# Two pairs of the first block taken plainly, weight buffers in another order, and four banks for the last pieces of a SwiGLU block

## The chip, the cores and the metric

The kernel runs on one core of one Trainium2 chip. The metric is the time of one execution on the device in microseconds (us); lower is better. All times of the trace are counted from the start of the profiled span.

## The reference

Two layers of a decoder trunk over 256 tokens of width 2048, in float32. Layer 0 mixes tokens with an mLSTM, layer 1 with a gated linear recurrence (RG-LRU); each layer then has a SwiGLU feed-forward block of width 5632.

```python
def swiglu(x, w_in, w_out):
    g, u = jnp.split(x @ w_in, 2, axis=-1)
    return (jax.nn.silu(g) * u) @ w_out

    h = x
    for layer in range(DEPTH):
        hn = rms_norm(h, norm_mix[layer])
        ...
        h = h + mix
        h = h + swiglu(rms_norm(h, norm_ffn[layer]), ffn_w_in[layer], ffn_w_out[layer])
    return rms_norm(h, norm_final)
```

## The kernel before, in words

**Products.** Every float32 operand is split into a high part and a rest, `hi` and `lo` (ACT casts `hi`, DVE subtracts to get `lo`: lines 229 and 230, or 208 and 209 in the mixers). One product is three matmuls, hi·hi, hi·lo and lo·hi (lines 725 to 727 in `ffn`, 281 to 283 in `linear_tok`).

**The feed-forward block.** `ffn` walks over 11 blocks `j` of 512 columns of the gate and of the up weights. Each block has 8 pairs `p` of k-tiles. Pairs 0, 1, 4 and 7 are plain: 8 products, so 24 matmuls of 128x512. Pairs 2, 3, 5 and 6 (`SEVENS`) use a scheme with seven products, 21 matmuls, for which DVE first makes sums of the weights (`sum`, lines 265 to 269) and two sets of operands are split (`whix`/`wlox` from the raw weights, `whit`/`wlot` from the sums). So a plain pair takes one buffer each of `whi` and `wlo`, a seven-product pair two of each. There are three buffers each of `raw`, `whi` and `wlo`, taken in turn by `four`, and one of `sum`. A cast into a buffer waits until the last matmul on what it held before is done.

**The output.** The result of block `j` is transposed (`tv`, line 780, split into `hh`), and multiplied with 512 rows of `ffn_w_out` in eight pieces (`outs`), 12 matmuls each, which are put between the matmuls of the following block from its pair 3 on. A piece uses one PSUM bank, `out`: ACT copies `h` into it (line 816), TensorE adds on top, ACT copies it back (line 823). In block 0 no pieces stand in between, since there is no block behind it.

**End of a layer.** Four pieces of block 9 are left over when block 10's products end. They run with the transposes of block 10 and the start of `project_out`, which multiplies block 10 with the last rows of `ffn_w_out` as a plain projection (`po0` to `po3`, lines 281 to 283), adds to `h` on DVE (line 458) and has ACT square the new columns (`junk`, line 334). Behind layer 0 the RG-LRU mixer follows: its first product `rec` (lines 298 to 300) needs its weights split by ACT (line 208) and DVE (line 209).

**What sets the order.** Within an engine the order is the program's, decided when the kernel is built by a scheduler that follows priorities (`tc.high_priority` draws work ahead) and the freeing of buffers. `PLACES` lists the buffers as memory pools in the order in which they are laid out; the pools of the next stage are laid over them from the front, and wait for whatever lies there.

## Time and profile before

| | |
|---|---|
| time, median of 3 runs | 2143.91 us (2141.2 to 2144.5) |
| profiled execution: its own time | 2139.45 us |
| profiled execution: span | 2137.6 us |
| TensorE (PE) busy | 2103.3 us, 98% of the span |
| VectorE (DVE) busy | 1595.6 us, 75% |
| ScalarE (ACT) busy | 1282.6 us, 60% |
| read from memory | 401.84 MB at 189 GB/s |

The profiled execution took 1.85 us more than its span, and 4.46 us less than the median of the runs. A row of a timeline gives the start in us, the duration, the engine, the line of the kernel, the operation and its operands, and in brackets how long the engine was idle before it and which instruction it then waited for. PE is TensorE's matmuls, PEld its weight loads, SPq the queue that issues transfers.

### The profile page before, as it was taken

To read this page: it belongs to the slowest core of one execution; us is meant where nothing else is said; L and a number is where in the kernel's file an instruction comes from. 1 tells how busy PE (TensorE), PEld (TensorE's weight loads), DVE (VectorE), ACT (ScalarE), POOL (GpSimd) and SP (SyncE) were. 2 spreads that over 40 slices of the span, in tenths; PEclk is the share of its full clock that TensorE was granted. 3 is DMA by queue.
4 is the path that set the end of the run, shared out by engine and by line. 5 is a ranking of instruction groups with operands and counts; after the bars stand their busy time and mean duration, and the time that the engine had idled before them with its cause. 6 is when DMAs were issued, how large, how long until landed. Compare 5 with 4: busy or idle time off the path is not lost.

```text
span 2137.6 us, 27324 instructions
## 1 busy us (share of the span) xinstructions
PE 2103.3 (98%) x10592; PEld 1774.7 (83%) x10592; DVE 1595.6 (75%) x1612; ACT 1282.6 (60%) x1458; POOL 43.0 (2%) x62
## 2 busy tenths in 40 slices
PE   9999999999999999999989999999999999999997
PEld 8988888777888888888879999777788888888886
DVE  6655556688788787878756786768877878887874
ACT  5344445556666656666654758655666666666664
POOL 0011110000000000000000000000000000000001
PEclk9999999999999999999999999999999999999999
DMA  6556656455665565665526665746566555566652
GB/s 212 168 160 183 179 179 223 160 197 197 204 215 193 187 206 179 213 219 195 181 97 195 191 189 186 228 156 203 192 210 221 191 184 196 194 206 211 207 181 105
DMA packets 211082, 405.73 MB, mean 190 GB/s; under 512 B 14520, under 2 KB 14728, under 8 KB 210824
## 3 DMA queue, kind: packets, MB, share of 16 engines
q1 hardware_dynamic: 210808, 402.94, 58.4%
q8 instruction: 83, 1.36, 0.3%
q10 hardware_dynamic: 144, 1.05, 0.1%
q14 instruction: 47, 0.39, 0.0%
HBM read 401.84 MB, written 2.10 MB: 189 GB/s over the span
## 4 chain that ended last, share of the span: by engine, by line
PE 91%; DVE 3%; ACT 3%; issue 1%; DMA 1%; SPq 0%; POOL 0%; ACTq 0%; POOLq 0%; DVEq 0%
PE P L725 7%; PE P L726 7%; PE P L727 7%; PE out L725 6%; PE out L727 6%; PE out L726 6%; PE Q L726 6%; PE Q L725 6%; PE Q L727 6%; PE po L282 3%; PE po L281 3%; PE po L283 3%; PE qk L298 1%; PE qk L299 1%; PE rec L300 1%; PE qk L300 1%
## 5 line engine op out<-in xcount | busy, mean ns | idle before, releaser
L209 DVE TENSOR_TENSOR wlo<-raw,whi 128x1024 fp32r<-128x1024 f32 (+1 forms) x225 | 273.0, 1218 | 183.8 <-ACT whi L208 182.8
L208 ACT CAST whi<-raw 128x1024 fp32r<-128x1024 f32 (+1 forms) x225 | 234.3, 1047 | 207.7 <-PE po L283 47.0
L230 DVE TENSOR_TENSOR wlot<-sum,whit 128x2048 fp32r<-128x2048 f32 x88 | 201.7, 2292 | 143.7 <-ACT whit L229 143.6
L725 PE MATMUL out<-whio,hh 128*128 128x512 f32 x640 | 249.9, 390 | 1.7 <-ACT out L816 1.7
L727 PE MATMUL out<-whio,hh 128*128 128x512 f32 x640 | 249.1, 389 | 0.0
L726 PE MATMUL out<-wloo,hh 128*128 128x512 f32 x640 | 249.1, 389 | 0.0
L823 ACT COPY h<-out 128x512 f32<-128x512 f32 x158 | 92.5, 586 | 259.0 <-PE out L727 258.8
L230 DVE TENSOR_TENSOR wlo<-raw,whi 128x2048 fp32r<-128x2048 f32 x96 | 220.2, 2296 | 32.1 <-ACT whi L229 31.2
L229 ACT CAST whio<-rawo 128x1024 fp32r<-128x1024 f32 x160 | 168.8, 1055 | 122.4 <-PE out L727 120.1
L229 ACT CAST whit<-sum 128x2048 fp32r<-128x2048 f32 x88 | 168.3, 1912 | 69.7 <-DVE sum L269 34.0
L229 ACT CAST whi<-raw 128x2048 fp32r<-128x2048 f32 x96 | 184.0, 1917 | 30.7 <-PE P L727 16.4
L230 DVE TENSOR_TENSOR wloo<-rawo,whio 128x1024 fp32r<-128x1024 f32 x160 | 193.3, 1221 | 8.8 <-ACT whio L229 8.3
L230 DVE TENSOR_TENSOR wlox<-raw,whix 128x1536 fp32r<-128x1536 f32 x88 | 154.5, 1756 | 50.3 <-ACT whix L229 49.9
L725 PEld LDWEIGHTS out<-whio,hh 128*128 128x128 f32 x640 | 120.1, 188 | 28.9 <-ACT out L816 4.0
L229 ACT CAST whix<-raw 128x1536 fp32r<-128x1536 f32 x88 | 130.4, 1482 | 20.5 <-PE Q L727 10.3
L727 PEld LDWEIGHTS out<-whio,hh 128*128 128x128 f32 x640 | 120.2, 188 | 25.2
L726 PEld LDWEIGHTS out<-wloo,hh 128*128 128x128 f32 x640 | 120.2, 188 | 24.9
L725 PE MATMUL Q<-whi,p_f 128*128 128x512 f32 x352 | 139.3, 396 | 0.9 <-DVE ds L764 0.9
L726 PE MATMUL Q<-wlo,p_f 128*128 128x512 f32 x352 | 137.5, 391 | 1.7 <-DVE wlo L230 1.7
L725 PE MATMUL P<-whi,p_f 128*128 128x512 f32 x352 | 137.8, 392 | 0.3 <-DVE ds L765 0.2
L727 PE MATMUL P<-whi,p_f 128*128 128x512 f32 x352 | 137.3, 390 | 0.0
L727 PE MATMUL Q<-whi,p_f 128*128 128x512 f32 x352 | 137.2, 390 | 0.0
(273 smaller groups left out, 4960.9 us busy)
## 6 DMA issues: line engine op xcount, KB each, us to landing
raw<-in_ffn_w_in_dram SPq DMA_DIRECT2D x352, 512.0 KB, 4.8
rawo<-in_ffn_w_out_dram SPq DMA_DIRECT2D x160, 512.0 KB, 4.2
raw<-in_m_w_in_dram SPq DMA_DIRECT2D x95, 512.0 KB, 3.8
raw<-in_r_w_in_dram SPq DMA_DIRECT2D x64, 512.0 KB, 4.1
raw<-in_m_w_out_dram SPq DMA_DIRECT2D x32, 512.0 KB, 3.8
raw<-in_r_w_out_dram SPq DMA_DIRECT2D x32, 512.0 KB, 4.3
raw<-in_ffn_w_out_dram SPq DMA_DIRECT2D x16, 512.0 KB, 6.3
gr<-in_r_gate_w_dram SPq DMA_DIRECT2D x8, 512.0 KB, 3.8
```

The costliest lines, as they stand in the source:

```text
L208: nc.scalar.copy(hi[:, i:i + step, 0:ncols], r)
L209: nc.vector.tensor_tensor(lo[:, i:i + step, 0:ncols], r, hi[:, i:i + step, 0:ncols].bitcast(F32), op=ALU.subtract)
L229: nc.scalar.copy(hi, src)
L230: nc.vector.tensor_tensor(lo, src, hi.bitcast(F32), op=ALU.subtract)
L281: nc.tensor.matmul(o, lhsT=ah[:, bs], rhs=hi, start=(k == 0), stop=False)
L282: nc.tensor.matmul(o, lhsT=ah[:, bs], rhs=lo, start=False, stop=False)
L283: nc.tensor.matmul(o, lhsT=al[:, bs], rhs=hi, start=False, stop=(k == nk - 1))
L300: nc.tensor.matmul(o, lhsT=lo, rhs=ah, start=False, stop=last, skip_group_check=True)
L725: nc.tensor.matmul(o, lhsT=a[0], rhs=b[0], start=start, stop=False, **kw)
L726: nc.tensor.matmul(o, lhsT=a[0], rhs=b[1], start=False, stop=False, **kw)
L727: nc.tensor.matmul(o, lhsT=a[1], rhs=b[0], start=False, stop=stop, **kw)
L823: nc.scalar.copy(hs, o)
```

## The change

Three edits. **(1)** In block 0 of each layer pairs 2 and 3 (`BOTH`) are taken plainly. The activations' three extra operands for each of the two (`more`, tags `m2` and `m3`) are made in `pair`, beside those of the seven products, during the projection ahead of the block. The pool of `h1` is opened only when `more` is closed, behind block 0; the early buffers change with it: pair 0 now takes `raw0`, `whi0` and `wlo0`, pair 1 takes memory of `h0` and `ds`. **(2)** `PLACES` is put in another order. **(3)** The pieces behind the first two left over, and all eight of block 10, are taken with `last=True`: weights come as one buffer of four k-tiles through `four` with two `raw` buffers in turn, the sum starts fresh in one of four banks (`acc`: Q5, P2, Q3, P4), and DVE adds it to `h`. This takes the place of `project_out`. The next norm is opened ahead of the pieces of block 10.

```diff
+BOTH = (2, 3)
...
     PLACES = (
-        "raw1", "raw2", "sum0", "whi1", "wlo1", "whi2", "rawo", "whio", "wloo", "wlo2", "raw0", "whi0", "wlo0",
+        "raw1", "raw2", "sum0", "rawo", "whio", "wloo", "wlo1", "whi1", "wlo2", "whi2", "raw0", "whi0", "wlo0",
     )
...
+    def is_plain(j, p):
+        return p not in SEVENS or j == 0 and p in BOTH
...
-            if p not in SEVENS:
+            if is_plain(j, p):
                 with tc.high_priority(offset=AHEAD):
                     both = halves(f"{j}_{p}", raw)
...
+            if p in BOTH:
+
+                nc.scalar.copy(c[:, 8, :], c[:, 0, :])
+                nc.vector.tensor_tensor(c[:, 9, :], c[:, 1, :], c[:, 2, :], op=ALU.subtract)
+                nc.vector.tensor_tensor(c[:, 10, :], c[:, 3, :], c[:, 0, :], op=ALU.subtract)
+                more = pool_of("more").tile([P, 2, 3, P], F32R, tag=f"m{p}", name=f"m{p}_{self.name}")
+                split(more[:, 0], more[:, 1], c[:, 8:11, :])
+                self.more[p] = more
...
-        early.update(raw="h0", whi="h1", wlo="ds")
+        early.update(raw=[None, "h0"], whi=[None, "ds"])
...
-            def load(q):
+            def load(q, last):
                 tiles.clear()
+                if last:
+                    raw = four("raw", f"o{j}{q}", F32, 2)
+                    for i in (0, 2):
+                        nc.sync.dma_start(raw[:, i:i + 2, :], wv[:, i:i + 2, q * NB:(q + 1) * NB])
+                    with tc.high_priority(offset=AHEAD):
+                        tiles.extend(halves(f"o{j}{q}", raw))
+                    return
...
-                o = pool_of("out").tile([P, NB], F32, tag="out", name=f"out{j}{q}{b}")
-
-
-                first = fresh.pop() if fresh else False
+                name = f"out{j}{q}{b}"
+                o = acc(name) if last else pool_of("out").tile([P, NB], F32, tag="out", name=name)
+
+
+                first = last or fresh.pop() if last or fresh else False
...
-        for left in range(len(work)):
-            work.pop(0)()
-            if left > 0 and turns:
+        turn["raw"] %= 2
+        for i, (piece, q, b) in enumerate(work):
+            piece(q, b, i >= 2)
+            if i >= len(work) - 2:
                 turns.pop(0)()
-        project_out(
-            ffn_w_out[layer][(NJ - 1) * NB:, :], 4, lambda k: (hi[:, k, :], lo[:, k, :]), nxt,
-        )
+        nxt.open()
+        for piece, q, b in late.pop()():
+            piece(q, b, True)
+            run_pending()
+            if q == 3 and nxt.lag:
+                nxt.store(b)
+            elif b == NT - 1:
+                pending.extend(nxt.parts(q))
```

**DVE, block 0 of layer 0.** The rows show line, operation, output and inputs, in DVE's order, from the start of block 0 on. `wlo0_1` is the rest of pair 1 of block 0, `wlox0_2`/`wlot0_2` those of pair 2 in the seven-product scheme, `sum0_2` its sums, `po3` the last projection ahead, `c_f06` the activations of pair 6. Before:

```order
L230 TENSOR_TENSOR wlo0_0_3651<-raw0_0_3647,whi0_0_3650 128x2048
L458 TENSOR_TENSOR h_73<-po3_0_3415,h_73 128x512
L458 TENSOR_TENSOR h_73<-po3_1_3416,h_73 128x512
L383 TENSOR_REDUCE ms_f0_3743<-ss_f0_154 128x2
L384 TENSOR_SCALAR ms_f0_3743<-ms_f0_3743 128x2
L265 TENSOR_TENSOR sum0_2_3751<-raw0_2_3748 128x1024
L268 TENSOR_TENSOR sum0_2_3751<-sum0_2_3751,raw0_2_3748 128x512
L230 TENSOR_TENSOR wlox0_2_3756<-raw0_2_3748,whix0_2_3755 128x1536
L269 TENSOR_TENSOR sum0_2_3751<-sum0_2_3751,raw0_2_3748 128x512
L416 TENSOR_TENSOR c_f06_3687<-c_f06_3687 128x256
```

And now:

```order
L485 TENSOR_TENSOR h_73<-po3_0_3430,h_73 128x512
L236 TENSOR_TENSOR wlo0_1_3715<-raw0_1_3711,whi0_1_3714 128x2048
L485 TENSOR_TENSOR h_73<-po3_1_3431,h_73 128x512
L392 TENSOR_REDUCE ms_f0_3758<-ss_f0_154 128x2
L393 TENSOR_SCALAR ms_f0_3758<-ms_f0_3758 128x2
L236 TENSOR_TENSOR wlo0_2_3767<-raw0_2_3763,whi0_2_3766 128x2048
L236 TENSOR_TENSOR wlo0_3_3798<-raw0_3_3794,whi0_3_3797 128x2048
L236 TENSOR_TENSOR wloo001_4168<-rawo001_4166,whio001_4167 128x1024
L429 TENSOR_TENSOR c_f06_3702<-c_f06_3702 128x256
L236 TENSOR_TENSOR wlo0_4_3829<-raw0_4_3825,whi0_4_3828 128x2048
```

The sums of pairs 2 and 3 are gone; the rests of pairs 2, 3 and 4 follow each other. Before, the rest of pair 4 stood behind all of the work for pairs 2 and 3.

**TensorE, end of layer 0.** `out920` is the piece of block 9 for output columns 1024 to 1535 and tokens 0 to 127, `out921` the same columns with tokens 128 to 255, `out930` the next columns; `tv` are the transposes of block 10. Before:

```order
L726 MATMUL out920_8607<-wloo921_8603,hh9_8123 128x512
L727 MATMUL out920_8607<-whio921_8602,hh9_8123 128x512
L780 MATMUL tv_8637<-ident_74,ds10_8124 128x128
L780 MATMUL tv_8671<-ident_74,ds10_8124 128x128
L725 MATMUL out921_8622<-whio920_8596,hh9_8123 128x512
L726 MATMUL out921_8622<-wloo920_8597,hh9_8123 128x512
L727 MATMUL out921_8622<-whio920_8596,hh9_8123 128x512
```

And now:

```order
L754 MATMUL out920_8616<-wloo921_8612,hh9_8132 128x512
L755 MATMUL out920_8616<-whio921_8611,hh9_8132 128x512
L755 MATMUL out930_8653<-whio93_8649,hh9_8132 128x512
L753 MATMUL out930_8653<-whio93_8649,hh9_8132 128x512
L754 MATMUL out930_8653<-wloo93_8650,hh9_8132 128x512
L755 MATMUL out930_8653<-whio93_8649,hh9_8132 128x512
L753 MATMUL out930_8653<-whio93_8649,hh9_8132 128x512
L754 MATMUL out930_8653<-wloo93_8650,hh9_8132 128x512
L753 MATMUL out921_8631<-whio920_8605,hh9_8132 128x512
L754 MATMUL out921_8631<-wloo920_8606,hh9_8132 128x512
```

Six matmuls of `out930`, which has a bank of its own, now stand between the two pieces that share the bank `out`; the first transposes stand behind the second of them.

**ACT, between layer 0 and the RG-LRU mixer.** `junk` are the squares of the new `h`, `x0_m1` to `x2_m1` the mixer's activations, and `whi0_8965` (now `whi0_8968`) is the first of the weights of `rec`; `whio103` is the last of `ffn_w_out`. Before:

```order
L334 ACTIVATE junk_8894,ss_m1_3596<-h_73 128x512
L334 ACTIVATE junk_8896,ss_m1_3596<-h_73 128x512
L354 ACTIVATE x2_m1_8875<-tr_m120_8876,cols0_106 128x256 x2
L354 ACTIVATE x2_m1_8875<-tr_m121_8885,cols0_106 128x256 x2
L334 ACTIVATE junk_9030,ss_m1_3596<-h_73 128x512
L334 ACTIVATE junk_9032,ss_m1_3596<-h_73 128x512
L208 CAST whi0_8965<-raw0_8963 128x1024
L208 CAST whi2_8995<-raw2_8993 128x1024
```

And now:

```order
L495 CAST hh10_8603<-tv_8688 128x512
L343 ACTIVATE junk_8774,ss_m1_3611<-h_73 128x512
L235 CAST whio103_8853<-rawo103_8850 128x2048
L210 CAST whi0_8968<-raw0_8966 128x1024
L210 CAST whi2_8998<-raw2_8996 128x1024
L210 CAST whi4_9063<-raw4_9061 128x1024
L363 ACTIVATE x0_m1_8755<-tr_m100_8756,cols0_106 128x256
L210 CAST whi6_9093<-raw6_9091 128x1024
```

The casts for `rec` stood behind the squares of the last columns of `h`; now they stand ahead of the mixer's first activations. In all TensorE has 12 more matmuls (10550 where there were 10538), DVE two and ACT six instructions fewer.

## Rows read from the trace of the kernel before

**Rows 1.** The page's first part: TensorE's busy time, its share of the span, and how many matmuls.

```profile
PE 2103.3 (98%) x10592; PEld 1774.7 (83%) x10592; DVE 1595.6 (75%) x1612; ACT 1282.6 (60%) x1458; POOL 43.0 (2%) x62
```

**Rows 2.** The waits of TensorE over the whole span: line, what was waited for, us in total, how many times, the longest.

```profile
PE rec L298 <- ACT whi L208: 3.9, 1, 3.9
...
PE P L725 <- ACT whix L229: 3.1, 2, 1.6
PE P L726 <- DVE wlox L230: 2.6, 2, 1.3
PE P L725 <- ACT whit L229: 2.2, 2, 1.1
PE Q L726 <- DVE wlo L230: 1.7, 2, 0.9
PE out L725 <- ACT out L816: 1.7, 3, 1.1
...
PE Q L725 <- DVE ds L764: 0.9, 2, 0.5
...
PE P L725 <- DVE ds L765: 0.2, 1, 0.2
```

**Rows 3.** TensorE's timeline in block 0 of layer 0, from pair 1 (409.30, 413.62) over the first matmul of pair 2 (414.21) to the last of pair 7 (450.62).

```profile
409.30 0.39 PE L726 MATMUL Q<-wlo,p_f 128*128 128x512 f32 x1
...
413.62 0.39 PE L727 MATMUL P<-whi,p_f 128*128 128x512 f32 x1
...
414.21 0.48 PE L725 MATMUL P<-whix,p_f 128*128 128x512 f32 x1
...
422.19 0.49 PE L725 MATMUL P<-whix,p_f 128*128 128x512 f32 x1 [1.56 <-ACT whix L229]
...
423.98 0.50 PE L726 MATMUL P<-wlox,p_f 128*128 128x512 f32 x1 [1.30 <-DVE wlox L230]
...
430.19 0.50 PE L726 MATMUL Q<-wlo,p_f 128*128 128x512 f32 x1 [0.85 <-DVE wlo L230]
...
442.96 0.50 PE L725 MATMUL P<-whit,p_f 128*128 128x512 f32 x1 [1.09 <-ACT whit L229]
...
450.62 0.39 PE L727 MATMUL P<-whi,p_f 128*128 128x512 f32 x1
```

**Rows 4.** DVE's groups from 402 to 1118 us (layer 0's feed-forward), by line and shape: shape, count, busy us, mean ns of one, idle time before them.

```profile
L230 DVE TENSOR_TENSOR wlo<-raw,whi 128x2048 fp32r<-128x2048 f32 x46 | 105.2, 2289 | 13.1 <-ACT whi L229 12.8
L230 DVE TENSOR_TENSOR wlot<-sum,whit 128x2048 fp32r<-128x2048 f32 x44 | 100.9, 2292 | 71.7 <-ACT whit L229 71.7
...
L230 DVE TENSOR_TENSOR wlox<-raw,whix 128x1536 fp32r<-128x1536 f32 x44 | 77.2, 1756 | 25.0 <-ACT whix L229 24.8
L265 DVE TENSOR_TENSOR sum<-raw 128x1024 f32<-128x1024 f32 x44 | 53.7, 1221 | 2.0 <-DMA raw<-in_ffn_w_in_dram 1.4
...
L269 DVE TENSOR_TENSOR sum<-sum,raw 128x512 f32<-128x512 f32 x44 | 30.4, 690 | 0.6
```

**Rows 5.** ACT's groups of the same stretch, in the same columns.

```profile
L229 ACT CAST whi<-raw 128x2048 fp32r<-128x2048 f32 x46 | 88.2, 1917 | 13.7 <-PE P L727 9.0 <-PE po L283 1.9 <-PE Q L727 1.2
...
L229 ACT CAST whit<-sum 128x2048 fp32r<-128x2048 f32 x44 | 84.1, 1912 | 34.9 <-DVE sum L269 17.1 <-PE P L727 8.9 <-PE Q L727 8.0
```

**Rows 6.** ACT's timeline in block 0 of layer 0: the first cast of pair 5.

```profile
420.66 1.47 ACT L229 CAST whix<-raw 128x1536 fp32r<-128x1536 f32 x1 [5.13 <-PE Q L727]
```

**Rows 7.** DVE's timeline in the mLSTM's output projection ahead of block 0, where the activations of pairs 2 and 3 are made.

```profile
363.09 0.29 DVE L419 TENSOR_TENSOR c_f<-c_f 128x128 f32<-128x128 f32 x1
...
365.38 1.08 DVE L230 TENSOR_TENSOR p_f<-c_f,p_f 128x896 fp32r<-128x896 f32 x1
...
375.61 1.23 DVE L209 TENSOR_TENSOR wlo<-raw,whi 128x1024 fp32r<-128x1024 f32 x1 [1.50 <-ACT whi L208]
```

**Rows 8.** TensorE's timeline at the end of layer 0.

```profile
1082.95 0.50 PE L725 MATMUL out<-whio,hh 128*128 128x512 f32 x1 [1.13 <-ACT out L816]
...
1087.21 0.50 PE L281 MATMUL po<-whi,hh 128*128 128x512 f32 x1 [0.56 <-ACT hh L468]
```

**Rows 9.** TensorE's timeline at the end of layer 1.

```profile
2096.67 0.55 PE L780 MATMUL tv<-ident,ds 128*128 128x128 f32 x3 [1.56 <-DVE ds L771]
```

**Rows 10.** The timeline of all engines where layer 1 begins, from the last matmul of layer 0's feed-forward to the first matmuls of `rec`.

```profile
1117.30 0.40 PE L283 MATMUL po<-whi,hh 128*128 128x512 f32 x1
...
1119.13 0.63 ACT L334 ACTIVATE junk<-h 128x512 f32<-128x512 f32 x1 [1.66 <-DVE h L458]
...
1120.51 3.88 ACT L208 CAST whi<-raw 128x1024 fp32r<-128x1024 f32 x4
...
1121.59 0.38 PE L298 MATMUL rec<-x_m,whi 128*128 128x256 f32 x1 [3.90 <-ACT whi L208]
...
1123.49 0.58 PE L300 MATMUL rec<-x_m,wlo 128*128 128x256 f32 x1 [0.66 <-DVE wlo L209]
```

**Rows 11.** Stretches around the same place: length, then busy us and instructions of PE, PEld, DVE, ACT and POOL, the clock that TensorE was granted (1.00 is 2.4 GHz, 0.5 is 1.2 GHz), DMA share and GB/s.

```profile
1117.60:1121.59 3.99, 0.10 (x1) 0.00 (x0) 2.36 (x7) 2.43 (x6) 0.51 (x1) 1.00 0.01 2
1121.60:1128.50 6.90, 6.25 (x28) 5.87 (x29) 5.02 (x6) 2.79 (x3) 0.18 (x1) 0.52 0.51 160
1128.50:1135.00 6.50, 6.50 (x57) 6.45 (x56) 4.09 (x6) 3.94 (x7) 0.00 (x0) 0.99 0.71 236
```

**Rows 12.** The page's transfers: the loads of `project_out`'s weights, count, KB each and median us from issue to landing.

```profile
raw<-in_ffn_w_out_dram SPq DMA_DIRECT2D x16, 512.0 KB, 6.3
```

More of the change, by code (lines that the diff above doesn't have):

```diff
@@ L222, in four @@
         if what in early:
-            return pool_of("f").tile([P, 4, NB], dtype, tag=early.pop(what), name=f"{what}{name}")
+            tag = early[what].pop(0)
+            if not early[what]:
+                early.pop(what)
+            if tag:
+                return pool_of("f").tile([P, 4, NB], dtype, tag=tag, name=f"{what}{name}")
         at = turn.get(what, 0)
@@ L396, with __init__ @@
     class NormPairs(Norm):
+        def __init__(self, *args, **kw):
+            super().__init__(*args, **kw)
+            self.more = {}
         def pair(self, p):
@@ L407, in pair @@
             place, tag = ("c", "c") if "c" in pools else ("rawo", "raw0")
-            c = pool_of(place).tile([P, 8, P], F32, tag=tag, name=f"c_{self.name}{p}")
+            c = pool_of(place).tile([P, 11 if place == "c" else 8, P], F32, tag=tag, name=f"c_{self.name}{p}")
             for k, sl in ((k0, slice(0, 2)), (k1, slice(2, 4))) if plain else ((k0, slice(1, 3)), (k1, slice(0, 4, 3))):
@@ L444, in plain @@
         def plain(self, p, f):
-            return [(self.x[p][:, 0, i, :], self.x[p][:, 1, i, :]) for i in (2 * f, 2 * f + 1, 4 + f)]
+            x = self.x[p]
+            if p not in self.more:
+                return [(x[:, 0, i, :], x[:, 1, i, :]) for i in (2 * f, 2 * f + 1, 4 + f)]
+            m = self.more[p]
+            return [
+                (t[:, 0, i, :], t[:, 1, i, :]) for t, i in (((x, 0), (x, 1), (m, 1)), ((x, 2), (m, 0), (m, 2)))[f]
+            ]
     def bc2(ap):
@@ L691, in opening @@
                 open_pool("x", "x_f0", side="right")
+                open_pool("more", "more_f0", side="right")
                 open_pool("c", "c_f0", side="right")
@@ L742, in inner @@
             for p, ops in pairs(w, j):
-                if p not in SEVENS:
+                if is_plain(j, p):
                     work = [
@@ L803, in load, with piece @@
                     tiles.extend((wh[:, k, :], wl[:, k, :]) for k in range(2))
-            def piece(q, b):
+            def piece(q, b, last=False):
                 if b == 0:
-                    load(q)
+                    load(q, last)
                 bs = slice(b * P, (b + 1) * P)
                 hs = h[:, b, q * NB:(q + 1) * NB]
-                o = pool_of("out").tile([P, NB], F32, tag="out", name=f"out{j}{q}{b}")
-                first = fresh.pop() if fresh else False
+                name = f"out{j}{q}{b}"
+                o = acc(name) if last else pool_of("out").tile([P, NB], F32, tag="out", name=name)
+                first = last or fresh.pop() if last or fresh else False
                 if not first:
@@ L823, in piece @@
                         nc.scalar.copy(hs, o)
-            return [lambda q=q, b=b: piece(q, b) for q in range(4) for b in range(NT)]
+            return [(piece, q, b) for q in range(4) for b in range(NT)]
         work, turns, late = [], [], []
@@ L831, in between @@
             if left == -2 - p % 2 and work:
-                work.pop(0)()
+                piece, *at = work.pop(0)
+                piece(*at)
             if left == 0 and p < 2:
@@ L841, in ffn @@
             v = inner(j, between)
-            both = fp.tile([P, 2, 4, T], F32R, tag=f"h{j % 2}", name=f"hh{j}")
+            if j == 0:
+                close_pools("more")
+                open_pool("h1", f"h1_f{layer}")
+            both = (pool_of("h1") if j % 2 else fp).tile([P, 2, 4, T], F32R, tag=f"h{j % 2}", name=f"hh{j}")
             hi, lo = both[:, 0], both[:, 1]
@@ L845, in ffn @@
             late.append(lambda j=j, hi=hi, lo=lo: outs(j, hi, lo))
-        for left in range(len(work)):
-            work.pop(0)()
-            if left > 0 and turns:
+        turn["raw"] %= 2
+        for i, (piece, q, b) in enumerate(work):
+            piece(q, b, i >= 2)
+            if i >= len(work) - 2:
                 turns.pop(0)()
-        project_out(
-            ffn_w_out[layer][(NJ - 1) * NB:, :], 4, lambda k: (hi[:, k, :], lo[:, k, :]), nxt,
-        )
+        nxt.open()
[6 more added lines that the diff above has]
+                pending.extend(nxt.parts(q))
     def close_ffn(*more):
-        close_pools("f", *reversed(PLACES), "out", "acc", *more)
+        close_pools("h1", "f", *reversed(PLACES), "out", "acc", *more)
         named.clear()
@@ L985, in opening @@
                 open_pool("x", "x_f1", side="right")
+                open_pool("more", "more_f1", side="right")
                 open_pool("c", "c_f1", side="right")
```

## The prediction, made before the changed kernel was run

> **What bounds the kernel now.** I read the page's busy times first, then TensorE's waits, then timelines around each wait, then stretches with the granted clock. TensorE is busy for 98% of the span [rows 1]: the kernel lasts as long as TensorE's matmuls take plus the time in which TensorE stands still or runs at half its clock. A saving therefore has to be a matmul less, or a stop less. The list of waits shows how little there is to take: its largest entries are one stop of 3.9 us ahead of `rec`, four kinds of stop on split operands with two of each (one in each layer), and some at the ends of the layers [rows 2]. The waits shown are not all that a stop costs, since the matmul behind a stop takes longer too. So I take each place by what elapsed against what its matmuls need. The pace is (413.62 - 409.30) / 19 = 0.227 us for a 128x512 matmul in an undisturbed stretch [rows 3].
>
> **Block 0 of each layer.** From the start of pair 2 to the start of the last matmul of pair 7 TensorE took 450.62 - 414.21 = 36.41 us; with the last matmul's own 0.23 that is 36.64. Its matmuls are 4 x 21 for the seven-product pairs and 2 x 24 for the plain ones, 132 x 0.227 = 29.97 us. So 6.67 us are lost, of which 1.56 + 1.30 + 0.85 + 1.09 = 4.80 are shown as waits [rows 3]. The cause is on DVE: for a seven-product pair it needs 1.22 + 0.69 + 0.69 + 1.76 + 2.29 = 6.65 us (the middle sum, whose row is left out, taken like the last one), for a plain one 2.29 [rows 4], while TensorE uses the pair up in 21 x 0.227 = 4.77 or 24 x 0.227 = 5.45 us. In later blocks the output pieces stand between, and give DVE time; in block 0 nothing does. The buffers tie it together: ACT waited 5.13 us for matmuls to give a `whi` buffer back, cast for 1.47 [rows 6], and the first matmul on the result started at once at 422.19 after a wait; the rest that DVE then makes (1.76) ends just ahead of 423.98, the next stop [rows 3, 4].
>
> With pairs 2 and 3 plain, DVE loses 2 x (6.65 - 2.29) = 8.7 us of work at this place, and ACT one cast of 1.9 and part of another for each pair [rows 5]. DVE's order has the rests of pairs 2, 3 and 4 directly behind each other, so pair 4's no longer stands behind the others' sums. Walking the new order with these durations from the same start: the rest of pair 2 is ready about 3.6 us ahead of TensorE, that of pair 3 about 7, that of pair 4 about 8, and the first casts of pair 5 wait only for pair 2 to be used up. The chain is tight again at pair 6, whose sums can be made only when the single `sum` buffer is given back by pair 5: there the cast of pair 7 (1.92) comes behind the cast of pair 6's sums (1.91), ends at about 438.9, and TensorE wants it at 438.3; with the next transposes behind it I leave 0.9 us of stops. The price is three more matmuls for each pair: 6 x 0.227 = 1.36 us in each layer. So each layer gains 6.67 - 1.36 - 0.9 = 4.4, and layer 1, whose waits at this place are the second halves of the same four entries [rows 2], the same: **-8.8 us** for both. The bounds: no stop left, -10.6; all of the gain eaten by new ones, 0.
>
> The extra operands are made earlier, in the mixers' output projections. For each pair they take DVE two subtractions of 0.29 and a split of 128x384 that is not in the trace: nothing at the least, and at the most the 1.08 of the 128x896 split [rows 7]; by size I take 0.5. ACT has a 128x128 copy and a cast of about the same size more. DVE stands idle there for 1.50 us ahead of each split of the weights, waiting for ACT's cast, which waits for TensorE [rows 7]; that idle time holds the 1.1 us. Without that cover it would be 4 x 1.1 = 4.4 us. I take 0.
>
> **The blocks behind it.** In blocks 1 and 2 TensorE waits 0.9 + 0.2 us for DVE's work on `ds` [rows 2]. TensorE's order does not change there, but the turns of the buffers do, and DVE reaches it less behind. I take half, **-0.6** (0 to -1.1).
>
> **The ends of the layers.** At the end of layer 0 TensorE waits 1.13 us for ACT's copy of `h` into the only `out` bank, and 0.56 for ACT's split of the transposes ahead of `po` [rows 8]; at the end of layer 1 it waits 1.56 for DVE's last product of the block ahead of the transposes [rows 9]. Two more waits on the copy, 1.7 - 1.13 = 0.57 together, are one at each end [rows 2]. Now six matmuls of `out930` (1.36 us), which has its own bank, stand between the pieces that share `out`, and the transposes stand behind `out921`, 12 matmuls (2.7 us) later. That covers the 1.13 and the 1.56. 1.13 + 0.56 + 1.56 + 0.57 = 3.8; I leave 0.3 at each end for what the shared bank still makes wait: **-3.2** (bounds 0, and -5 with the slower matmuls behind each stop).
>
> **The start of layer 1.** The last matmul of layer 0 starts at 1117.30; DVE adds it to `h`, ACT squares twice, and only then, from 1120.51, does ACT cast the weights of `rec`: the casts stand behind the squares in ACT's queue. TensorE starts at 1121.59, after a wait of 3.90 us, and stops once more for 0.66 [rows 10]. Then comes a second loss: in the 6.9 us from 1121.60 its granted clock is 0.52, that is, it falls from 2.4 to 1.2 GHz right after the stop, and only 28 matmuls start, where the 6.5 us behind, at a clock of 0.99, have 57 [rows 11]. At that pace the 28 would take 28 x 6.50 / 57 = 3.19 us, so 3.7 us are lost, the 0.66 among them. Together 7.6 us. With the new order of the pools the buffers of `rec` lie over ones that are free early, and ACT's order has `rec`'s casts ahead of the mixer's activations and of the last squares. I expect `rec` to start directly and the clock to stay up. What is new: the bank of one of its products is the one that the last piece but two used, and waits for DVE's add (0.69, as DVE's sums over 512 columns [rows 4]); I set 0.4 for it. **-7.2** (bounds 0 and -7.6).
>
> The end of the program, from the last matmul on, is the same chain of add, squares, scaling and store, and nothing of it moves.
>
> **Sum.** -8.8 - 0.6 - 3.2 - 7.2 = -19.8. From the profiled execution's 2139.45 that gives 2119.6; the runs shown have a median 4.46 above that, so I put the changed kernel at 2143.91 - 19.8, **2124.0 us**, 0.93% faster.
>
> **Rivals.**
> *The clock does not always fall.* Only one execution is profiled. If in the timed runs the stop of 3.9 us is often passed at full clock, they have less to win: -19.8 + 3.7 - 0.66 = -16.8, 2127.1. For it speaks the spread of the runs of before, 3.3 us; against it that the fall begins right behind the stop. The Trainium skill ("TensorE: Matmul & The Clock Gate", Part 1: The HAM clock gate) has the gate judge TensorE's activity on a grid of windows that runs freely and isn't started by the kernel, so that the same stop can cost a different amount from run to run; one profile can't show it.
> *The wait ahead of `rec` stays.* The casts need weights that have landed in buffers which the new order only promises early. If they come late, the 7.2 us are not won: -12.6, 2131.3. It decides if the first cast ends later than about 1117 on the old scale.
> *Block 0 gains nothing.* If pairs 5 to 7 wait for as long as pairs 2 to 5 did, since there the same DVE work is squeezed behind the same buffers: -11.0, 2132.9. Against it speaks that two such pairs are left where there were four.
> *No change.* The 20 last pieces (ten in each layer) each end with a DVE add. If a piece had to wait for the add ahead of it, 0.69 and some 0.3 for refilling, 20 x 1.0 = 20 us would eat all: 2144. With four banks a bank comes round after three other pieces, 8.2 us, so the add must be late by that much.
> *Slower.* The last weights go through two `raw` buffers instead of three. One use of a buffer is 6.3 us for the load [rows 12], 1.92 for the cast and 2.29 for the rest, 10.5 us, and two buffers give one load in 5.25 us; TensorE uses one up in 24 x 0.227 = 5.45. It holds by 0.2 us. If loads took 11.5 us, each of the ten would be late by 2.4, 24 us in all, and the kernel would be slower by over 0.2%: 2148 or more. Against it: the 6.3 are taken where several loads are issued at once, and two buffers can be filled ahead.
>
> **How the numbers follow.** Forecast 0.66; clock 0.13; wait ahead of `rec` 0.08; block 0 without gain 0.05; no change 0.04; slower 0.04. The range goes from 2117 (all of the bounds taken, -24.3, would be 2119.6, and the runs of before spread by 3.3 us) to 2133, which takes in the first three rivals. What a measurement can tell from no change is 0.2%, 4.3 us: faster by more than that 0.92, within 0.04, slower 0.04.
>
> **What would show it.** In the profile after: no waits on `whix` and `wlox` of pairs 2 to 5 in block 0, at most about 0.6 us on pair 7; the last matmul of block 0 some 4.4 us earlier in both layers; no wait of `rec` on ACT, and a granted clock of 1.00 in the 7 us behind its start; waits on the copy into `out` of 0.3 each; 12 more matmuls. I am wrong if `rec` still waits, if block 0 ends less than 3 us earlier, or if the last pieces wait for weights.

## The result, and the profile of the changed kernel

The changed kernel takes 2117.84 us (median of 4 runs, 2115.55 to 2118.39), the kernel before, run beside it, 2143.05 us (2141.2 to 2144.5): 25.2 us less, a ratio of 0.9881 with a 95% interval of 0.9864 to 0.9898. In a second set, with more runs of the kernel before (see below), the ratio was 0.9893 (0.9879 to 0.9906): the changed kernel took the same there (2117.57), the kernel before 2.6 us less (2140.49). The profiled execution of the changed kernel has a span of 2116.6 us, 21.0 less than the one of before. The forecast was 2124.0, with a range of 2117 to 2133: the time lies at the lower end, 0.8 us above its bound.

The page's first part for the changed kernel, as in [rows 1]:

```profile
PE 2099.8 (99%) x10604; PEld 1777.5 (84%) x10604; DVE 1584.5 (75%) x1610; ACT 1274.6 (60%) x1452; POOL 43.2 (2%) x62
```

TensorE is busy for 3.5 us less, though it has 12 matmuls more: a matmul behind a stop takes longer (0.48 to 0.50 us for 0.39 in [rows 3]), and at the lower clock fewer start in the same busy time (28 in 6.25 us for 57 in 6.50, [rows 11]). The whole list of TensorE's waits in the changed kernel (line, what was waited for, us, times, longest); the line numbers are those of the changed file, 753 to 755 for 725 to 727, 210 and 235 for ACT's casts in 208 and 229, 307 for 298, 485 for 458:

```profile
PE qk L307 <- ACT x_m L363: 3.3, 1, 3.3
PE P L753 <- ACT whi L235: 1.6, 2, 0.8
PE warm L142 <- DVE mhalf L144: 1.1, 1, 1.1
PE po L291 <- DVE wlo L211: 0.9, 2, 0.7
PE po L290 <- ACT whi L210: 0.3, 1, 0.3
PE Q L753 <- DVE h L485: 0.2, 1, 0.2
```

Of the eight entries of [rows 2] not one is left. New are the 1.6 us on `whi` (twice, once in each layer) and 0.2 on `h`. Block 0 of layer 0 on TensorE's timeline, to be set beside [rows 3]: the first matmul of pair 2, the one wait, the last matmul of block 0:

```profile
414.66 0.48 PE L753 MATMUL Q<-whi,p_f 128*128 128x512 f32 x1
...
439.79 0.50 PE L753 MATMUL P<-whi,p_f 128*128 128x512 f32 x1 [0.81 <-ACT whi L235]
...
446.97 0.39 PE L755 MATMUL P<-whi,p_f 128*128 128x512 f32 x1
```

From the first to the last of these it is 32.31 us, where [rows 3] give 36.41. The start of `rec`, beside [rows 10], and the stretch of 6.9 us behind it, beside [rows 11]:

```profile
1109.90 0.39 PE L755 MATMUL out<-whio,hh 128*128 128x512 f32 x1
1110.12 0.28 PE L307 MATMUL rec<-x_m,whi 128*128 128x256 f32 x1
1110.24 0.28 PE L308 MATMUL rec<-x_m,whi 128*128 128x256 f32 x1
```

```profile
1110.10:1117.00 6.90, 6.90 (x59) 6.82 (x58) 3.85 (x9) 3.60 (x8) 0.70 (x1) 1.00 0.05 12
```

`rec` starts 0.22 us behind the start of the last matmul of the feed-forward, and the granted clock stays at 1.00: 59 matmuls in 6.9 us, where before 28 were started.

The same stretches of TensorE's timeline, each from the start of a matmul to the start of another, for four profiles of the kernel before and two of the changed one (the later ones are from the experiments). "Block 0" goes from the first matmul of pair 2 to the first of block 1; "to `rec`" from there to the first of `rec`; "to layer 1's FFN" from there to the first of its pair 0; "to the last" from the first matmul of block 1 in layer 1 to the last of all.

| us | before | again | third | fourth | changed | again |
|---|---|---|---|---|---|---|
| block 0, layer 0 | 36.68 | 37.49 | 36.69 | 37.77 | 32.54 | 32.45 |
| to `rec` | 670.70 | 670.84 | 671.23 | 671.38 | 662.93 | 663.01 |
| to layer 1's FFN | 294.39 | 293.56 | 294.18 | 296.21 | 292.21 | 292.20 |
| block 0, layer 1 | 36.69 | 37.36 | 36.72 | 37.69 | 32.54 | 32.78 |
| to the last | 663.34 | 663.49 | 665.13 | 663.70 | 659.65 | 659.73 |
| span | 2137.6 | 2137.7 | 2140.0 | 2141.9 | 2116.6 | 2115.9 |

Two things stand in it. Every stretch of the table is shorter in the changed kernel; of what the table leaves out, pairs 0 and 1 of layer 1 take 12.2 us for 11.7. And the kernel before differs from execution to execution by up to 4.3 us in its span, while the changed one's two agree within 0.7.

### The profile page after: what moved, and what is told of

It reads as the page before. It is cut to its first block, busy times and chain, and to the rows that moved or that the text cites. A ratio compares the mean times of both kernels' runs of the same rounds, so it can differ in the third digit from the quotient of the medians.

```text
span 2116.6 us, 27325 instructions
## 1 busy us (share of the span) xinstructions
PE 2099.8 (99%) x10604; PEld 1777.5 (84%) x10604; DVE 1584.5 (75%) x1610; ACT 1274.6 (60%) x1452; POOL 43.2 (2%) x62
## 4 chain that ended last, share of the span: by engine, by line
PE 96%; ACT 2%; DVE 1%; issue 1%; DMA 0%; SPq 0%; ACTq 0%; POOLq 0%; POOL 0%; DVEq 0%
PE P L753 8%; PE out L753 8%; PE P L755 8%; PE P L754 8%; PE out L754 8%; PE out L755 8%; PE Q L754 7%; PE Q L755 7%; PE Q L753 7%; PE po L291 2%; PE po L292 2%; PE po L290 2%; PE qk L307 1%; PE qk L308 1%; PE qk L309 1%; PE v L290 1%
## 5 line engine op out<-in xcount | busy, mean ns | idle before, releaser
L236 DVE TENSOR_TENSOR wlot<-sum,whit 128x2048 fp32r<-128x2048 f32 x84 | 192.5, 2292 | 147.3 <-ACT whit L235 147.3
L753 PE MATMUL out<-whio,hh 128*128 128x512 f32 x704 | 275.0, 391 | 0.0
L754 PE MATMUL out<-wloo,hh 128*128 128x512 f32 x704 | 274.3, 390 | 0.0
L755 PE MATMUL out<-whio,hh 128*128 128x512 f32 x704 | 273.3, 389 | 0.0
L235 ACT CAST whio<-rawo 128x1024 fp32r<-128x1024 f32 (+1 forms) x166 | 183.7, 1106 | 126.5 <-PE out L755 119.1
L236 DVE TENSOR_TENSOR wlo<-raw,whi 128x2048 fp32r<-128x2048 f32 x92 | 210.3, 2288 | 32.0 <-ACT whi L235 31.4
L236 DVE TENSOR_TENSOR wloo<-rawo,whio 128x1024 fp32r<-128x1024 f32 (+1 forms) x166 | 210.9, 1282 | 3.6 <-ACT whio L235 3.0
L753 PEld LDWEIGHTS out<-whio,hh 128*128 128x128 f32 x704 | 132.2, 188 | 28.9 <-ACT out L855 0.9
L755 PEld LDWEIGHTS out<-whio,hh 128*128 128x128 f32 x704 | 132.2, 188 | 27.8
L754 PEld LDWEIGHTS out<-wloo,hh 128*128 128x128 f32 x704 | 132.2, 188 | 27.2
L753 PE MATMUL P<-whi,p_f 128*128 128x512 f32 x364 | 141.9, 390 | 1.6 <-ACT whi L235 1.6
L755 PE MATMUL P<-whi,p_f 128*128 128x512 f32 x364 | 141.9, 390 | 0.0
L754 PE MATMUL P<-wlo,p_f 128*128 128x512 f32 x364 | 141.6, 389 | 0.0
```

Of the source, the lines that this page charges most:

```text
L235: nc.scalar.copy(hi, src)
L236: nc.vector.tensor_tensor(lo, src, hi.bitcast(F32), op=ALU.subtract)
L753: nc.tensor.matmul(o, lhsT=a[0], rhs=b[0], start=start, stop=False, **kw)
L754: nc.tensor.matmul(o, lhsT=a[0], rhs=b[1], start=False, stop=False, **kw)
L755: nc.tensor.matmul(o, lhsT=a[1], rhs=b[0], start=False, stop=stop, **kw)
```

## The experiments

**Without each part.** Three kernels, each the changed one without one of its three parts, on one chip. The theory to be tested was that each part buys the stops at its own place and nothing else.

```diff
-BOTH = (2, 3)
+BOTH = ()
```

> The changed kernel without its first part: no pair of block 0 is taken plainly in place of the seven-product scheme (BOTH is empty). The parts add up (my theory): between the two profiles block 0 ended 4.14 us earlier in each layer, so this kernel should take 8.3 us more than the changed one, about 2126, with TensorE's stops in block 0 back (some 4.8 us shown in each layer) and the rest as in the changed kernel. Rival, the turns of the buffers tie block 0 to blocks 1 and 2: then the stops on ds in those blocks (1.3 us in each layer) come back too, and it takes about 11 us more.

It took 2131.9 us (2131.1 to 2132.4), against before a ratio of 0.9957 (0.9944 to 0.9969), so 14 us more than the changed kernel; by the profiles 12.7. All of it lies in block 0, which took 39.20 us in layer 0 and 39.00 in layer 1: not 4.1 but 6.7 and 6.5 us more than the changed kernel, and 2.4 more than the kernel before in its first profile. The other stretches stayed (to `rec` 663.3, to the last 659.8), so the rival fell too, and with it the additive reading: the waits in block 0 of layer 0 are other ones than before.

```profile
PE P L753 <- ACT whit L235: 2.0, 2, 1.4
PE Q L753 <- ACT whi L235: 1.3, 1, 1.3
PE Q L753 <- ACT c_f L423: 1.0, 1, 1.0
PE P L754 <- DVE wlot L236: 0.5, 1, 0.5
PE P L753 <- ACT whix L235: 0.4, 1, 0.4
```

Here and in layer 1 the granted clock fell behind the first stops (length, busy us of PE, PEld, DVE, ACT, POOL, clock, DMA share, GB/s):

```profile
424.20:427.60 3.40, 3.34 (x8) 2.48 (x8) 3.40 (x4) 0.00 (x0) 0.00 (x0) 0.50 0.03 12
```

A part of the 2.4 us is this fall: beside the executions of the kernel before whose clock fell in block 0 too (37.4 to 37.8 us, the table above) it is 1.3 to 1.7 us more. So the other early buffers, which the first part brings along, make block 0 slower than it was as long as its pairs 2 and 3 take two buffers each. The diff has one buffer fewer for an early `wlo`, which may be the reason; that was not tried apart.

```diff
     PLACES = (
-        "raw1", "raw2", "sum0", "rawo", "whio", "wloo", "wlo1", "whi1", "wlo2", "whi2", "raw0", "whi0", "wlo0",
+        "raw1", "raw2", "sum0", "whi1", "wlo1", "whi2", "rawo", "whio", "wloo", "wlo2", "raw0", "whi0", "wlo0",
     )
```

> The changed kernel with the old order of the memory pools. My theory: the order of the pools alone decides where ACT's casts for rec stand, so rec waits for them again (about 4 us) and TensorE runs the first 7 us behind it at half its clock: 6 to 7.6 us more than the changed kernel, about 2124 to 2125.5. Rival, the new last pieces make the buffers free early enough by themselves: no stop, same time as the changed kernel. Second rival, the clock does not fall each time: the stop without the half clock, about 4 us more.

2122.9 us (2122.2 to 2124.5), ratio 0.9916 (0.9903 to 0.9930): 5 us more than the changed kernel. `rec` waits again, though for less than in [rows 10], and the clock falls to its lower level once more:

```profile
PE rec L307 <- ACT whi L210: 2.5, 1, 2.5
PE rec L309 <- DVE wlo L211: 1.0, 1, 1.0
```

```profile
1115.70:1119.10 3.40, 3.40 (x18) 3.40 (x17) 2.57 (x3) 0.12 (x1) 0.00 (x0) 0.50 0.85 265
```

18 matmuls start in 3.4 us at a clock of 0.50. The stop is shorter than before (2.5 us for 3.9), and the fall lasts 3.4 us, half of that in [rows 11]. ACT's casts for `rec` stand behind the last squares again:

```profile
1111.32 0.63 ACT L343 ACTIVATE junk<-h 128x512 f32<-128x512 f32 x1 [1.79 <-DVE h L860]
...
1111.95 3.88 ACT L210 CAST whi<-raw 128x1024 fp32r<-128x1024 f32 x4
```

The order of the pools decides where the casts stand, as the theory said; the size was less than its 6 to 7.6, because stop and fall were both smaller.

```diff
-        turn["raw"] %= 2
-        for i, (piece, q, b) in enumerate(work):
-            piece(q, b, i >= 2)
-            if i >= len(work) - 2:
+        for left in range(len(work)):
+            piece, *at = work.pop(0)
+            piece(*at)
+            if left > 0 and turns:
                 turns.pop(0)()
...
-        for piece, q, b in late.pop()():
+        project_out(
+            ffn_w_out[layer][(NJ - 1) * NB:, :], 4, lambda k: (hi[:, k, :], lo[:, k, :]), nxt,
+        )
```

> The changed kernel with the old end of a layer: the left-over pieces through the one bank with ACT's copies, then the projection po. My theory: the stops at the two ends come back, 2.8 us of lost time in layer 0 and 2.6 in layer 1, 5.4 us more than the changed kernel, about 2123; rec still starts without a stop. Rival: without the early squares of h the casts for rec come late again, then 9 to 13 us more.

2122.4 us (2121.7 to 2123.4), ratio 0.9911 (0.9896 to 0.9927); by the profiles 5.0 us more than the changed kernel. The waits of the two ends, of layer 0 (the first two rows) and of layer 1, are back with the numbers of [rows 8, 9]:

```profile
PE out L753 <- ACT out L855: 1.4, 2, 1.1
PE po L290 <- ACT hh L495: 0.6, 1, 0.6
...
PE tv L808 <- DVE ds L799: 1.6, 1, 1.6
```

and `rec` still starts without a stop. This part is what the theory said, and independent of the order of the pools.

**The changed kernel and single parts beside the kernel before,** on one chip. The first has no edit.

> The changed kernel once more, beside runs of the kernel before on the same chip, so that the single parts of this call can be set against it. If the 25.2 us of the first result are what the stops cost in timed runs (21.0 between the two profiles, the rest because the granted clock falls at more of before's stops in other executions), the ratio should be 0.988 to 0.990 again; if the first result was one lucky set of runs, nearer to 0.9906, the 19.8 us of the forecast or the 21.0 of the profiles.

2117.6 us (2117.4 to 2118.8) against 2140.5: ratio 0.9893 (0.9879 to 0.9906), 22.9 us. Its interval and that of the first result overlap between 0.9879 and 0.9898, that is 22 to 26 us. The profiles' 21.0 us lies within the second interval alone, the forecast's 19.8 in neither.

`only_both` has the old `PLACES` and the old end of a layer, as in the two diffs above, and keeps the first part.

> Only the first part: pairs 2 and 3 of block 0 plain, with the early buffers that go with it; the old order of the pools and the old ends of the layers. My theory: 8 to 9 us faster than before (4.1 to 4.4 us in each layer's block 0), and the stops on ds in blocks 1 and 2 (1.3 us in each layer by elapsed time) go too, since they were absent in all three kernels that kept only the early buffers in common: 11 us, ratio 0.995. Rival: the ds stops belong to one of the other two parts and stay: 8.5 us, ratio 0.996. The stop ahead of rec and those at the ends stay.

2129.2 us, ratio 0.9949 (0.9936 to 0.9961): 11.3 us less than before. Block 0 took 32.86 and 32.50 us, as in the changed kernel, and the list of waits has no `ds` ahead of the products of blocks 1 and 2 any more (the `ds` below is the one at layer 1's end), while `rec` and both ends are as before:

```profile
PE rec L307 <- ACT whi L210: 3.9, 1, 3.9
...
PE P L753 <- ACT whi L235: 1.9, 2, 1.1
PE out L753 <- ACT out L855: 1.7, 3, 1.1
PE tv L808 <- DVE ds L799: 1.6, 1, 1.6
```

So the stops on `ds` in blocks 1 and 2 went with the first part; `no_both`, which lacked them too, had its early buffers without the plain pairs, so it is most likely these, and the turns of the buffers that they shift, that remove them.

`only_places` is the kernel before with the new `PLACES` and no other edit.

> The kernel before with nothing but the new order of the memory pools. My theory: rec starts without a stop and at full clock, and loses 1.7 us of that again because its 256-column matmuls keep the slower of their two paces (0.118 us instead of 0.113) that the fall of the clock had reset: about 6 us faster, ratio 0.997; the stops in blocks 0, 1 and 2 and at the ends stay. Rival: without the early squares the wait only moves, and the gain is under 2 us.

2135.5 us, ratio 0.9975 (0.9964 to 0.9985): 5.0 us less than before. There is no wait of `rec`, and block 0's and the ends' waits stay:

```profile
PE P L725 <- ACT whix L229: 3.1, 2, 1.6
...
PE out L725 <- ACT out L816: 1.9, 4, 1.1
PE tv L780 <- DVE ds L771: 1.6, 1, 1.6
PE P L725 <- DVE ds L765: 1.2, 2, 0.9
```

ACT casts the first weights of `rec` at 1100.46 us here, and not behind the last squares as in [rows 10]. To `rec` it took 666.62 us, 4.1 less than in the first profile of before, and from there to layer 1's feed-forward 292.13, 2.3 less, as in the changed kernel; block 0 was longer (37.70 and 38.17), since the clock fell in both in this execution. The single parts together, 11.3 + 5.0, and the 4.8 by which `no_last`, on another chip, was slower than the changed kernel give 21 us, where the whole gave 22.9: within the intervals the parts add, as long as the early buffers go with the plain pairs.

**The pace of the 256-column matmuls.** From `rec` on the changed kernel won 2.2 us, and not the 3.7 that [rows 11] show as lost. The matmuls of 128x256 of `rec` and of `gb`, the product behind it, 192 each, stand 0.1178 us apart in it, for the first 45 us (the rows above: 1110.12, 1110.24), and 0.1133 in the kernel before, at the same granted clock. `extra_one` issues one matmul more ahead of them; it changes no result.

```diff
         for k, hi, lo in stream(w, c0, nk):
             ah, al = act(k)
+            if name == "rec0" and k == 0:
+                nc.tensor.matmul(ps[0].rearrange("p f t -> p (f t)"), lhsT=ah[:, 0:P], rhs=hi, start=True, stop=False, skip_group_check=True)
```

> The changed kernel with one matmul of 512 columns more, ahead of rec's first, into a bank that rec then starts afresh (its result is not used). In the profiles the 256-column matmuls run at 0.113 or at 0.118 us, and change from one to the other where single 512-column matmuls stand between them. Theory: the pace hangs on how the stream is lined up when a stretch starts, so one matmul more can put rec, which ran at 0.118 in its first 45 us, on 0.113, and rec ends 1.5 us earlier. Rival: the pace hangs on where the operands lie, or on what the other engines do; then rec stays at 0.118 and 0.23 us are lost.

Its one run took 2117.1 us, and from `rec` to layer 1's feed-forward 292.29 us, no gain. But the pace did change, up to the transposes:

```profile
1111.65 0.28 PE L307 MATMUL rec<-x_m,whi 128*128 128x256 f32 x1
1111.76 0.28 PE L308 MATMUL rec<-x_m,whi 128*128 128x256 f32 x1
1111.87 0.28 PE L309 MATMUL rec<-x_m,wlo 128*128 128x256 f32 x1
1111.99 0.28 PE L307 MATMUL rec<-x_m,whi 128*128 128x256 f32 x1
...
1113.01 1.04 PE L359 MATMUL tr_m<-ident,h 128*128 128x128 f32 x8
1113.88 0.60 PE L403 MATMUL bc_m<-dg_m,ones 128*128 128x256 f32 x2
...
1114.43 0.28 PE L308 MATMUL rec<-x_m,whi 128*128 128x256 f32 x1
1114.55 0.28 PE L309 MATMUL rec<-x_m,wlo 128*128 128x256 f32 x1
1114.67 0.28 PE L307 MATMUL rec<-x_m,whi 128*128 128x256 f32 x1
1114.79 0.28 PE L308 MATMUL rec<-x_m,whi 128*128 128x256 f32 x1
```

Three steps ahead of them take 0.34 us, three behind them 0.36. The operands lie where they lay, and only a matmul was added, so the place of the operands alone doesn't set the pace. The 1.5 us were missed, since most of the 384 matmuls stand behind the broadcast. `extra_two` has the same edit and writes the broadcast behind the transposes twice:

```diff
                 pb = misc(f"bc_{self.name}")
+                if self.name == "m1":
+                    nc.tensor.matmul(pb[:, 0:T], lhsT=ones, rhs=dg.rearrange("p b t -> p (b t)"), start=True, stop=True)
                 nc.tensor.matmul(pb[:, 0:T], lhsT=ones, rhs=dg.rearrange("p b t -> p (b t)"), start=True, stop=True)
```

> As the kernel with one matmul more, and in addition the mixer's broadcast of rstd (bc, a product with ones) written twice into the same bank. In the kernel with one matmul more rec ran at 0.113 us up to the transposes and the broadcast, and at 0.118 behind them. Theory (the pace hangs on how the stream is lined up): rec runs at 0.113 on both sides, the stretch from rec to the second feed-forward gets 1.5 us shorter. Rival: transposes and broadcast always leave the slower pace, whatever their number; then as before.

Now the pace stays at 0.113 behind the broadcast too. The stretch of 10 us from 1125, of the changed kernel and then of `extra_two`:

```profile
1125.00:1135.00 10.00, 10.00 (x88) 10.00 (x87) 5.18 (x7) 4.03 (x4) 0.00 (x0) 1.00 0.70 179
```

```profile
1125.00:1135.00 10.00, 10.00 (x91) 10.00 (x90) 5.52 (x7) 4.02 (x4) 0.00 (x0) 1.00 0.64 192
```

88 and 91 matmuls. From `rec` to layer 1's feed-forward it took 291.21 us, 1.0 less than the changed kernel: two thirds of what was expected. The time of its one run, 2117.7, can't show that against the others' spread, so it isn't shown to be a better kernel.

**One buffer for the last loads,** to test the forecast's slower rival:

```diff
-                    raw = four("raw", f"o{j}{q}", F32, 2)
+                    raw = four("raw", f"o{j}{q}", F32, 1)
```

> The changed kernel with the last pieces' weights through one raw buffer in place of two. The slower rival of the prediction counted 10.5 us for one use of a buffer (6.3 for the load, 1.92 and 2.29 for the split), against 5.45 us in which TensorE uses a load up. If that is right, each load but the first two of a layer is some 5 us late here: 8 x 5 less the 10 us or so by which the first ones are ahead in each layer, so 20 to 35 us slower than the changed kernel. If the loads alone take the 4.3 us that the page of after has for them, 8.5 us for a use: 3 us late each, 10 to 20 us slower. If the loads are so far ahead that their buffers don't matter, the same time as the changed kernel.

2122.3 us (2120.4 to 2125.8), ratio 0.9907 (0.9890 to 0.9925): some 5 us slower than the changed kernel, less than each of the expectations with a number, and not the same time either. New in its waits are these:

```profile
PE out L754 <- DVE wloo L236: 1.6, 1, 1.6
PE tr_m L357 <- DVE h L860: 1.3, 1, 1.3
PE out L753 <- ACT out L855: 1.2, 2, 0.6
...
PE out L753 <- ACT whio L235: 0.4, 1, 0.4
```

0.4 + 1.6 us are waits for a split weight, both at layer 1's end, the second with a fall of the clock behind it. The 1.3 stand behind one, at layer 0's end: DVE's add came behind a rest of weights that itself had waited 3.15 us for ACT's cast. The 0.6 us on ACT's copy at each end were not followed further. DVE's rests of the last two loads of layer 1, and TensorE's stop on the last:

```profile
2095.59 2.29 DVE L236 TENSOR_TENSOR wloo<-rawo,whio 128x2048 fp32r<-128x2048 f32 x1 [3.62 <-ACT whio L235]
...
2105.22 2.29 DVE L236 TENSOR_TENSOR wloo<-rawo,whio 128x2048 fp32r<-128x2048 f32 x1 [2.37 <-ACT whio L235]
...
2107.57 0.50 PE L754 MATMUL out<-wloo,hh 128*128 128x512 f32 x1 [1.59 <-DVE wloo L236]
```

From the end of one load's rest to that of the next it is 9.6 us here, and 9.6 to 11.7 over the five loads of both layers, 10.2 on average. So the rival's 10.5 us for one use of a buffer was right, and each load behind the first does fall back by some 5 us. But the first of the five was split 15.5 us ahead of TensorE's first matmul on it, in both layers, where the expectation allowed some 10, and the other four use this lead up: the last split ends 0.5 us ahead of its use in layer 0 and 2.3 us behind it in layer 1. In the changed kernel, with two buffers, it ends 6.5 and 5.1 us ahead.

**The kernel before, three times more.** No edit.

> The kernel before, unchanged, profiled once more. The profiled execution of before took 2139.45 us, 4.5 less than the median of its runs, and that of after 0.5 more than its own. If before has places that cost a different time from one execution to the next (the stop ahead of rec and the half clock behind it, or the pace of the 256-column matmuls, 0.113 or 0.118 us), this profile should be nearer 2143 and show which place differs by 2 to 4 us; if the profile was only lucky in many small ways, no single place differs by more than 1 us.

> The kernel before, profiled a third time. In the first two profiles the granted clock fell in other places: behind the stop ahead of rec in both, in block 0 of both layers in the second alone. Theory (the same stops cost a fall in some executions and none in others): again another set of falls, and where one falls at a stop of block 0, that block is 0.7 to 1.5 us longer than 36.7. Rival: the falls belong to one chip or to one day; then the set of the second profile, 37.4 us for each block 0.

> The kernel before, profiled a fourth time, right behind the third, on the same chip. As for the third: if each execution draws its own set of falls, this one differs from the third; if the set belongs to the chip, it is the third's.

The three profiled executions took 2139.5, 2141.9 and 2143.8 us. The second, which was expected nearer 2143, is as fast as the first, and no stretch of it differs by more than 0.8 us. The clock fell behind the stop ahead of `rec` in all four profiles of before, and in block 0 of both layers in the second and the fourth alone. The same 3.4 us of block 0 in the second, third and fourth:

```profile
424.05:427.45 3.40, 3.40 (x10) 2.63 (x9) 2.92 (x3) 1.53 (x1) 0.00 (x0) 0.50 0.02 5
```

```profile
424.05:427.45 3.40, 3.22 (x13) 2.37 (x14) 3.36 (x4) 2.18 (x4) 0.00 (x0) 1.00 0.11 40
```

```profile
424.05:427.45 3.40, 3.40 (x10) 2.68 (x9) 3.04 (x3) 1.10 (x1) 0.00 (x0) 0.53 0.02 5
```

Third and fourth were taken on the same chip, one behind the other: the set of falls belongs to the execution, not to the chip. There are two sets in the four, the third having the first's and the fourth the second's, and they go with the program's start: the clock was at its lower level there for 6.8 us in the first and third (from 9.1 and 9.4 us on), and for 3.4 us in the second and fourth (from 11.0 and 10.8). Each fall in block 0 made it 0.7 to 1.1 us longer (the table). Two more places differ. In the third a copy into the bank `out` came late at layer 1's end, behind a stop of 1.42 us that the others don't have; in the fourth `rec` ran at the slower pace (0.1178) even behind a fall, and the stretch took 296.2.

## Why the prediction held, and where its terms were off

The direction, the places and the range were right; the forecast was 5.4 us short in the first result and 3.1 in the second. The first result's 25.2 us is more than the 24.3 of all bounds taken together; that the time still lies in the range is due to the 3.3 us allowed for the spread, which is luck in part. (2143.91 - 19.8 is 2124.1 and 0.92%, not 2124.0 and 0.93%.) Set against the two first profiles, term by term:

| | forecast | measured | from |
|---|---|---|---|
| block 0, both layers | -8.8 | -8.3 | table: 36.68 to 32.54, 36.69 to 32.54 |
| blocks behind it (`ds`) | -0.6 | -2.4 | 1.3 and 1.1 us of elapsed time |
| ends of the layers | -3.2 | -5.2 | the rest of "to `rec`" and "to the last" |
| `rec`: stop and clock | -7.2 | -6.1 | 3.9 in "to `rec`", 2.2 behind it |
| not forecast | 0 | +0.9 | start +0.5, pairs 0 and 1 of layer 1 +0.5 |
| sum | -19.8 | -21.1 | span: -21.0, the rest is rounding |

Of the +0.9, the start of the program differs by up to 1.0 us between executions of one kernel, so its 0.5 isn't shown to be the change's. The 0.5 in pairs 0 and 1 of layer 1 belong to the change: all kernels with the new early buffers have them, behind a stop of 0.18 us on DVE's add to `h`. The forecast has no term for this place.

**Block 0** was sized well, by the same working: three more matmuls for each pair, and a stop left at pair 7, 0.81 us on the cast of `whi`, where 0.6 was written. Its mechanism is more bound up with the early buffers than the forecast said: `no_both` shows them to cost 1.3 to 1.7 us in each layer when the plain pairs aren't there, and the clock fell in both.

**The blocks behind it and the ends of the layers** were mis-sized for one reason. For block 0 I had taken the elapsed time against what the matmuls need; for these I took the waits that the list shows, and left part of them standing besides. The waits are only a part of what a stop costs: at the end of layer 0 1.13 + 0.56 + 0.27 us of waits stood for 2.8 us of elapsed time, in blocks 1 and 2 0.7 for 1.3. And no stop stayed at the shared bank, where I left 0.3 at each end. Halving the `ds` term had no reason in the trace; `only_both` shows that all of it goes with the first part.

**The start of `rec`** went as told: no stop, clock at 1.00. The 0.4 us left for the bank was not needed. What was missing is the slower pace, which takes 384 x 0.0045 = 1.7 us of the 3.9 + 3.7 back, and which no row shown ahead of the prediction could tell, since [rows 11] have only the stretch at the faster one.

**The rivals.** That the clock does not fall each time was priced with the wrong sign. `rec`'s stop made it fall in all four profiles of before; but in two of four it fell in block 0 as well, so other executions of before are slower than the one that I summed against, and the change takes that away too. That is a part of the 2 to 4 us by which the timed gain exceeds the profiled one: before's four spans have a mean of 2139.3 us, 1.7 above the first, the changed kernel's two 2116.2, and 23.1 us between them is what the profiles show. Of the 1.7 us the falls in block 0 are 0.9; the rest lies in other places, above all the third's late copy and the fourth's slower pace. On this the Trainium skill ("TensorE: Matmul & The Clock Gate", Part 1: The HAM clock gate) says that the gate's grid runs freely and is not started by the kernel; the four profiles agree, with the same two stops (1.56 and 1.29 us) behind which the clock fell at 424 us in two executions, and did not in the other two. I had drawn from it only the case that costs the change something. Whether the larger gain of the first result, 25.2 us, has a further cause stays open.

The wait ahead of `rec`, block 0 without gain, no change and slower did not come about. For the last, `one_raw` bears out the price, 10.2 us for one use of a buffer where 10.5 was written. What kept the loads in time is not the margin of 0.2 us but what the rival named against itself: they are filled ahead, the first of them by some 15 us.

## What to carry to other kernels

Size a stop by the time that elapsed between two instructions against the number of instructions between them at the undisturbed pace, and not by the wait that a list shows: here the waits held half to three quarters of it. A stop of TensorE behind which the clock falls costs more than itself, and the clock doesn't fall in each execution: two stops of block 0 made it fall in two of four, for 1.5 to 2.1 us over both layers. So profile the kernel before more than once before working against a single span. What is to run first in the next stage belongs on memory that comes free early, since the order of the pools moved ACT's casts, and with them 5 us, without a single instruction more.

## What the runs showed of the hardware that was not expected

Matmuls of 128x256 in an unbroken stream run at one of two paces, 0.1133 or 0.1178 us from start to start, at a granted clock of 1.00 in both, and keep it over hundreds of matmuls until something else stands between them. The same product, `rec`, had the faster one in three profiles of before, behind a fall of the clock, and the slower one in the fourth and in both of the changed kernel. In the other kernels too it was the slower one wherever `rec` started without a stop (`no_both`, `no_last`, `only_places`, `one_raw`), and the faster one behind a stop and a fall (`no_places`, `only_both`). One matmul more ahead of it, or the broadcast written twice, moved it from one to the other. So what ran ahead of a stretch decides its pace, by a mechanism that no run here shows. For the 128x512 matmuls of the feed-forward blocks no second pace is seen in the stretches compared (0.227 us).
